# Two transformer blocks on one core: where the operands of the feed-forward matmuls lie in the on-chip memory

## The chip, the core and the metric

One core of a Trainium2 chip runs the whole program. The metric is the device time of one execution in microseconds. The kernel before took 2065.55 us (median of 3 runs, 2063.72 to 2067.26).

## The reference

A sequence of 256 positions with 1,024 features goes through two blocks in float32. The first block has an RWKV-7 and an RG-LRU branch, a cross attention and a feed-forward with a short convolution (`conv_ffn`). The second block runs twice (two layers), each with a gated feed-forward, a token mixing of three attention forms, a cross attention and a second gated feed-forward. What the change touches are the feed-forwards:

```
def swiglu(h, w13, w2):
    gate, up = jnp.split(h @ w13, 2, axis=-1)
    return (jax.nn.silu(gate) * up) @ w2

x = x + 0.5 * rms_norm_2(swiglu(rms_norm_2(x, g0), w13, w2), g1)   # D_MODEL 1024, D_FF 2816
```

There are four of these gated feed-forwards (two per layer) and one `conv_ffn` of the same sizes.

## The kernel before, in words

**Products in three parts.** Every large product is made of three matmuls in a reduced-precision form of float32: an operand is split into a high part (a cast on ScalarE, line 209) and a low part (a subtraction on VectorE, line 210), and `mm3` (lines 240 to 244) adds high x high, high x low and low x high in the accumulator. In the profile the lines 242, 243 and 244 are these three. A name with h or l at its end is a high or low part; in `out<-in,in` the moving operand comes first and the stationary one second.

**Weights.** `weights` (213) loads a raw tile of 128 x 1,024 floats from SP's queue and splits it into `wh` and `wl`, in pool `wp` with three buffers each. `wcols` (229) gives the eight row tiles of a column block.

**Feed-forward** (`ffn`, 405). `norm_T` (355) normalises and transposes the activations into eight slices xt of 128 x 256 (high and low), held in four of the ten 4,096-byte buffers of pool `sl4`. Then comes a loop over 11 hidden blocks j of 256 columns: `proj_fm` (255) makes gate and up, 48 matmuls of 256 columns each, with the weights stationary and xt moving; `hidden` applies the gate; the result is split into hh and hl. One step later `down` (276) multiplies the hidden block j-1, now stationary in pieces of 128 x 128, with the down weights, now moving with 512 columns: 24 matmuls a block into four accumulators. The last three of the 22 down rows keep their weights in a pool `tail` of their own (281 to 303) and are multiplied together. `fill` (two key/value projections of the memory for the next cross attention, `kv_job` 1007) gives TensorE work while the activations are normalised.

**Cross attention** (`cross`, 488) has its own pool: kv (8 buffers, keys, values and, later, the heads' outputs), `gap0` (64 bytes), queries, p, `gap1` (384 bytes), pt; the pool `tail` for its down projection (`down_all`, 305) is opened behind it. The heads' outputs are the stationary operand of that down projection. In the mixing block (`mix2`, 1356) the stationary operand of the down projection is `mh`/`ml`, in `sl4` (`merge`, 173).

**Order of work.** The instructions of each engine are ordered by a scheduler that follows the program's order and priorities with a model of the time; waits follow from the data and from the reuse of buffers. Nothing in the order is written by hand around the change. Pools are laid behind one another in the order in which they are opened, and tiles in a pool in the order in which their names first appear.

**Places.** Modulo 256 bytes: the `sl4` buffers start at 0. Line 119 puts a pad of 64 bytes behind them, so that `wp` and the pools opened later (`ff`, `tail`, `cr`) start at 64; `mix2` starts its pool with a pad of 448. Tiles of the loops are multiples of 1,024 bytes long, so distances are the same for every buffer of a name. So xt (in `sl4`) is 64 bytes below its weights or, counted upwards, 192 above; hh and hl (in `ff`) are at the same place as the down weights; mh and ml are 64 bytes below theirs; the heads' outputs in `cross` are level with the weights in `wp`, and 64 above those in `tail`, which start 448 bytes on.

Of the kernel before, what the change touches and what calls it, by code (L numbers as in the profile page):

```python
# [110 lines left out]
class Core:  # L111
# [290 lines left out]
        return xs  # L402


    def ffn(self, xs, gsrc, w_in, w_out, hidden, fill=None):
        xt = self.norm_T(xs, gsrc)
        if fill:
            self.parts = PK
            fill()
        self.parts = PF  # L410
        pend = []
        with self.pool("ff", 3) as pool, self.pool("tail", FTAIL) as tail, self.pool("raws", 7) as raws:
            self.phase(pool)
            acc, step = self.down_steps(w_out, 2 * NJ, tail, FTAIL)
            for j in range(NJ + 1):
                self.raws = raws if j else self.wp
                if j < NJ:
                    bg = self.proj_fm(self.wcols(w_in, j * 256, 256), xt)
                    bu = self.proj_fm(self.wcols(w_in, FF + j * 256, 256), xt)
                    hd = hidden(j, bg, bu)  # L420
                    p = Pair(self.R("hh", [128, 2, T], F32R), self.R("hl", [128, 2, T], F32R))
                    self.split(hd, p.h, p.l)
                    pend.append(p)
                if j:
                    for i in range(2):
                        step(2 * (j - 1) + i, pend[j - 1][:, i, :])
        self.raws = self.wp
        return acc
# [59 lines left out]
    def cross(self, xs, gx, w_q, w_o, mt, w_kv, raw, mid=None, ntail=TAIL):  # L488

        nc = self.nc  # L490
        self.parts = PC
        R = self.R
        xt = self.norm_T(xs, gx)
        after = self.last_copy
        kv = {}

        def get(i):

            got = []
            if i in raw:  # L500
                for r in raw[i]:
                    p = Pair(R("kvh", [128, 2, T], F32R, 8), R("kvl", [128, 2, T], F32R, 8))
                    with self.tc.issue_after(after):
                        self.split(r, p.h, p.l)
                    got.append([p[:, 0, :], p[:, 1, :]])
            else:
                got = [self.fm_pair(b, "kv", 8) for b in self.kv_chunk(mt, w_kv, i)]
            if i < 4:
                kv[i] = got[0]
            else:  # L510
                for j in range(2):
                    kv[2 * i - 4 + j] = [got[0][j], got[1][j]]

        outs = {}
        sc, pt = {}, {}

        def scores(h):
            if h == 0:
                R("gap0", [128, 16], bufs=1)
            q = self.fm_pair(self.proj_fm(self.wcols(w_q, h * 256, 256), xt), "cq", 2)  # L520
            b = self.bank("c")
            v = b.rearrange("p (a c) -> p a c", a=2)
            for t in range(2):
                for i in range(2):
                    self.mm3(v[:, t, :], q[i][:, t * 128:(t + 1) * 128], kv[h][i], t == 0 and i == 0, t == 1 and i == 1)
            p, rc = self.softmax_bank(v, 2, 256 ** -0.5, R("p", [128, 2, T], bufs=4))
            for t in range(2):
                nc.vector.tensor_scalar(out=p[:, t, :], in0=p[:, t, :], scalar1=rc[:, t:t + 1], scalar2=None,
                                        op0=ALU.mult)
            sc[h] = p  # L530

        def values(h):
            p = sc[h]
            b = self.bank("c")
            for kt in range(2):
                for t in range(2):
                    o = kt * T + t * 128
                    nc.tensor.transpose(b[:, o:o + 128], p[:, t, kt * 128:(kt + 1) * 128], self.ident)
            if h == 0:
                R("gap1", [128, 96], bufs=1)  # L540
            pt = self.fm_pair(b, "pt", 2)
            b = self.bank("c")
            for i in range(2):
                for kt in range(2):
                    self.mm3(b[:, i * T:(i + 1) * T], kv[4 + h][kt][:, i * 128:(i + 1) * 128], pt[kt],
                             i == 0 and kt == 0, i == 1 and kt == 1)
            outs[h] = self.fm_pair(b, "kv", 8)

        for i in range(6):
            if i not in raw:  # L550
                get(i)
        for h in range(4 + LAG):
            if h < 4:
                for i in (h, 4 + h // 2):
                    if i in raw and (i < 4 or h % 2 == 0):
                        get(i)
                scores(h)
            if h >= LAG:
                values(h - LAG)
        if mid:  # L560
            mid()
        return self.down_all([outs[h][i] for h in range(4) for i in range(2)], w_o, ntail)
# [456 lines left out]
    def run(self, out):  # L1019
        a, nc = self.a, self.nc  # L1020
        n2 = a["cross_norms_2"]
        side = ExitStack()
        mem = {}

        def open_side():
            self.rawp = side.enter_context(self.pool("raw", side="right"))
            self.pad(self.rawp, 224)
            mem["R"] = self.mkR(side.enter_context(self.pool("mt", side="right")))

        def early(pool):  # L1030
            mem["mt"] = self.norm_T(self.load_x(a["mem"][0]), a["norm_mem_g"][0])
            mem["raw"] = {i: [pool.tile([128, 2, T], F32, name="raw_b1%d" % i)] for i in range(NEARLY)}
            self.kv_job(mem["mt"], a["w_ckv"][0], mem["raw"])(8)

        def prepare(l):

            mt = self.mem_T(a["mem_2"][0], n2[l, 2], mem["R"])
            rt = lambda n: self.rawp.tile([128, 2, T], F32, tag=n, name=n)
            raw = {i: [rt("raw%d%d" % (i, j)) for j in range(1 if i < 4 else 2)] for i in range(5)}
            mem.update(mt=mt, raw=raw, fill=self.kv_job(mt, a["cross_wkv_2"][l], raw))  # L1040

        fill = lambda n: mem["fill"](n)

        def start_ffn():
            fill(2)
            self.rope_tables()

        with self.pool("b1") as pool:
            with self.pool("gt") as gp:
                xs = self.mix1(gp, lambda names: self.load_const(names, pool), lambda: early(pool), open_side)  # L1050
            with self.pool("cr") as cp:
                self.phase(cp)
                acc = self.cross(xs, a["norm_x_g"][0], a["w_cq"][0], a["w_co"][0], mem["mt"], a["w_ckv"][0],
                                 mem["raw"], mid=lambda: prepare(0))
            xs = self.residual(xs, acc)
            acc = self.ffn(xs, a["norm_ffn_g"][0], a["w_ffn_in"][0], a["w_ffn_out"][0], self.conv_hidden,
                           start_ffn)
        xs = self.final_norm(self.residual(xs, acc), a["norm_final_g"])
        with self.pool("b2") as pool:
            self.load_const(["ret"], pool)  # L1060
            for l in range(2):
                acc = self.ffn(xs, a["ffn1_norms_2"][l, 0], a["ffn1_w13_2"][l], a["ffn1_w2_2"][l], self.swiglu_hidden,
                               lambda: fill(2))
                xs = self.residual(xs, acc, a["ffn1_norms_2"][l, 1], 0.5)
                acc = self.mix2(l, xs, lambda: fill(6))
                xs = self.residual(xs, acc, a["mix_norms_2"][l, 1])
                with self.pool("cr") as cp:
                    self.phase(cp)
                    acc = self.cross(xs, n2[l, 0], a["cross_wq_2"][l], a["cross_wo_2"][l], mem["mt"],
                                     a["cross_wkv_2"][l], mem["raw"], mid=(lambda: prepare(1)) if l == 0 else side.close, ntail=TAILS[l])  # L1070
                xs = self.residual(xs, acc, n2[l, 1])
                acc = self.ffn(xs, a["ffn2_norms_2"][l, 0], a["ffn2_w13_2"][l], a["ffn2_w2_2"][l], self.swiglu_hidden,
                               (lambda: fill(2)) if l == 0 else None)
                xs = self.residual(xs, acc, a["ffn2_norms_2"][l, 1], 0.5)
        for t in range(2):
            for h in range(2):
                s = slice(h * 512, (h + 1) * 512)
                nc.sync.dma_start(out=out[t * 128:(t + 1) * 128, s], in_=xs[t][:, s])
# [377 lines left out]
```

## Time and profile before

| | |
|---|---|
| median of 3 runs | 2065.55 us |
| profiled execution | 2068.93 us |
| its span, first to last instruction | 2067.2 us |
| TensorE matmul busy | 2006.2 us (97%) |
| VectorE, ScalarE busy | 1320.1 us (64%), 1093.7 us (53%) |
| mean granted TensorE clock | 0.991 |

Busy times of TensorE are made from reported starts and modelled ends: matmuls are pipelined, and a reported duration is longer than the distance to the next start. The distance between starts is what a matmul costs in a row of them. The timeline gives the start of each instruction, its duration, and the idle time before it in brackets where there is any.

### The profile page before, as it was taken

What the parts mean: (1) busy time and instruction counts of PE and PEld (TensorE: products, weight loads), DVE (VectorE), ACT (ScalarE), POOL (GpSimd) and SP (SyncE); (2) the same over time, 40 slices, a digit from 0 to 9 for tenths busy, and PEclk for the clock granted to TensorE, in tenths of its full rate; (3) what the DMA queues carried; (4) which work ended last, traced back from release to release, by engine and by line L of the source; (5) the groups of instructions that cost most, each with busy time, mean ns of one, the idle gap of its engine ahead of it and who ended that gap; (6) DMA issues with size and microseconds to landing.
All of it is one profiled execution on the core that took longest, in us unless ns stands there. A gap on an engine that the chain in (4) does not pass through costs nothing.

```text
span 2067.2 us, 36137 instructions
## 1 busy us (share of the span) xinstructions
PE 2006.2 (97%) x14508; PEld 1843.3 (89%) x14508; DVE 1320.1 (64%) x2183; ACT 1093.7 (53%) x2014; POOL 45.6 (2%) x65
## 2 busy tenths in 40 slices
PE   7999999999999999999999999999999999998998
PEld 6989978899999998789988999999987799888997
DVE  6896567766675556765667555755577656665555
ACT  5763245655564455654456544644466544554444
POOL 0000000000000001000000000000000000000000
PEclk9999999999999999999999999999999999999999
DMA  6432255666666655436655666656644456545663
GB/s 199 145 119 83 93 183 188 221 184 191 188 218 193 185 163 154 136 108 184 200 194 194 212 189 190 208 175 192 190 121 148 123 163 185 192 154 174 193 191 105
DMA packets 259033, 352.92 MB, mean 171 GB/s; under 512 B 12336, under 2 KB 214448, under 8 KB 258864
## 3 DMA queue, kind: packets, MB, share of 16 engines
q1 hardware_dynamic: 258864, 350.60, 55.1%
q8 instruction: 114, 1.87, 0.4%
q14 instruction: 55, 0.45, 0.1%
HBM read 349.50 MB, written 1.05 MB: 170 GB/s over the span
## 4 chain that ended last, share of the span: by engine, by line
PE 86%; DVE 5%; DMA 4%; ACT 3%; issue 1%; POOL 0%; SPq 0%; DVEq 0%; POOLq 0%; ACTq 0%
PE bp L242 20%; PE bp L243 20%; PE bp L244 20%; PE acc L242 6%; PE acc L243 6%; PE acc L244 6%; PE a L247 3%; DVE wl L210 2%; ACT wh L209 2%; PE bc L247 1%; DMA raw<-in_w_in_dram 1%; PE bc L1131 1%; PE bc L368 1%; DMA raw<-in_cross_wkv_dram 1%; DMA g<-in_cross_norms_dram 1%
## 5 line engine op out<-in xcount | busy, mean ns | idle before, releaser
L210 DVE TENSOR_TENSOR wl<-raw,wh 128x512 fp32r<-128x512 f32 (+2 forms) x1082 | 796.7, 773 | 532.9 <-ACT wh L209 520.8
L209 ACT CAST wh<-raw 128x512 fp32r<-128x512 f32 (+2 forms) x1082 | 699.7, 688 | 713.2 <-PE bp L243 496.8
L242 PE MATMUL bp<-xth,wh 128*128 128x256 f32 x2704 | 763.8, 283 | 8.3 <-ACT xth L209 3.8
L244 PE MATMUL bp<-xth,wl 128*128 128x256 f32 x2704 | 760.7, 282 | 5.4 <-DVE wl L210 5.4
L243 PE MATMUL bp<-xtl,wh 128*128 128x256 f32 x2704 | 761.3, 282 | 2.9 <-DVE xtl L210 2.9
L242 PEld LDWEIGHTS bp<-xth,wh 128*128 128x128 f32 x2704 | 513.2, 190 | 19.4 <-ACT xth L209 6.5
L244 PEld LDWEIGHTS bp<-xth,wl 128*128 128x128 f32 x2704 | 515.5, 191 | 11.3 <-DVE wl L210 6.4
L243 PEld LDWEIGHTS bp<-xtl,wh 128*128 128x128 f32 x2704 | 512.8, 190 | 6.8 <-DVE xtl L210 4.1
L243 PE MATMUL acc<-wl,hh 128*128 128x512 f32 x440 | 171.8, 390 | 0.0
L244 PE MATMUL acc<-wh,hl 128*128 128x512 f32 x440 | 170.5, 390 | 0.0
L242 PE MATMUL acc<-wh,hh 128*128 128x512 f32 x440 | 142.0, 391 | 0.0
L242 PE MATMUL bp<-wh,xth 128*128 128x512 f32 (+1 forms) x256 | 98.7, 400 | 2.3 <-DVE tmd L1126 1.4
L243 PE MATMUL bp<-wl,xth 128*128 128x512 f32 (+1 forms) x256 | 100.5, 396 | 0.0
L244 PE MATMUL bp<-wh,xtl 128*128 128x512 f32 (+1 forms) x256 | 99.2, 393 | 0.0
L243 PEld LDWEIGHTS acc<-wl,hh 128*128 128x128 f32 x440 | 82.7, 188 | 14.4
L244 PEld LDWEIGHTS acc<-wh,hl 128*128 128x128 f32 x440 | 82.6, 188 | 14.5
L242 PEld LDWEIGHTS acc<-wh,hh 128*128 128x128 f32 x440 | 79.1, 188 | 13.3
L343 POOL TENSOR_TENSOR rr<-rv,mhalf 128x1 f32<-128x1 f32 x46 | 30.2, 658 | 1656.8 <-DVE rv L341 1656.4
L242 PEld LDWEIGHTS bp<-wh,xth 128*128 128x128 f32 x256 | 47.3, 188 | 13.3 <-ACT tmd L1276 2.1
L243 PEld LDWEIGHTS bp<-wl,xth 128*128 128x128 f32 x256 | 48.2, 188 | 9.2 <-DVE wl L210 0.8
L244 PEld LDWEIGHTS bp<-wh,xtl 128*128 128x128 f32 x256 | 48.2, 188 | 8.4
L244 PE MATMUL bp<-bh,wl 128*128 128x256 f32 x192 | 54.0, 281 | 0.0
(377 smaller groups left out, 2582.7 us busy)
## 6 DMA issues: line engine op xcount, KB each, us to landing
raw<-in_ffn_w_dram SPq DMA_DIRECT2D x264, 512.0 KB, 4.4
raw<-in_w_in_dram SPq DMA_DIRECT2D x134, 512.0 KB, 3.8
raw<-in_w_ffn_in_dram SPq DMA_DIRECT2D x44, 512.0 KB, 4.6
raw<-in_cross_wkv_dram SPq DMA_DIRECT2D x32, 512.0 KB, 4.2
raw<-in_w_branch_dram SPq DMA_DIRECT2D x24, 512.0 KB, 3.9
raw<-in_w_ffn_out_dram SPq DMA_DIRECT2D x22, 512.0 KB, 4.2
raw<-in_w_ckv_dram SPq DMA_DIRECT2D x16, 512.0 KB, 4.3
raw<-in_w_out_dram SPq DMA_DIRECT2D x16, 512.0 KB, 4.3
```

The costliest lines, as they stand in the source:

```text
L209: first = self.nc.scalar.copy(out=h, in_=src)
L210: self.nc.vector.tensor_tensor(out=l, in0=src, in1=h.bitcast(F32), op=ALU.subtract)
L242: mm(out, a.h, b.h, start=start, stop=False, skip_group_check=True)
L243: mm(out, a.h, b.l, start=False, stop=False, skip_group_check=True)
L244: mm(out, a.l, b.h, start=False, stop=stop, skip_group_check=True)
L247: self.nc.tensor.matmul(out, a, b, start=start, stop=stop, skip_group_check=True)
L343: nc.gpsimd.tensor_tensor(out=r, in0=v, in1=self.mhalf[:, :1], op=ALU.pow)
L368: nc.tensor.transpose(b[:, j * 128:(j + 1) * 128], xn[:, k * 128:(k + 1) * 128], self.ident)
L1131: self.nc.tensor.transpose(b[0:s.shape[1], i * 128:(i + 1) * 128], s, self.ident)
```

## The change

Three things. The gated feed-forwards get their xt in four buffers of a pool of their own (4,352 bytes each, opened ahead of the hidden buffers), starting 208, 200, 176 and 184 bytes further than the weights modulo 256 (first feed-forward of layer 0 and of layer 1, second feed-forward of layer 0 and of layer 1). In all five feed-forwards 192 bytes are put ahead of hh and hl and 64 behind them, so that hh and hl stand 64 bytes below the down weights and all that follows keeps its place modulo 256. In the three cross attentions 64 bytes are put behind pt, so that the tail weights of their down projection move up by 64 bytes. No instruction of the computation is added or taken away.

```diff
-    def ffn(self, xs, gsrc, w_in, w_out, hidden, fill=None):
-        xt = self.norm_T(xs, gsrc)
+    def ffn(self, xs, gsrc, w_in, w_out, hidden, fill=None, off=None):
+
+        if off is not None:
+            with self.pool("xt") as pool:
+                tile = lambda n: pool.tile([128, 1088], F32R, name=n)[:, off // 4:off // 4 + 1024].rearrange(
+                    "p (k c) -> p k c", k=4)
+                xt = [Pair(tile("fxh%d" % i), tile("fxl%d" % i)) for i in range(2)]
+                return self.ffn_on(self.norm_T(xs, gsrc, xt), w_in, w_out, hidden, fill)
+        return self.ffn_on(self.norm_T(xs, gsrc), w_in, w_out, hidden, fill)
+
+    def ffn_on(self, xt, w_in, w_out, hidden, fill):
...
                     hd = hidden(j, bg, bu)
+                    if j == 0:
+                        self.R("gap0", [128, 48], bufs=1)
                     p = Pair(self.R("hh", [128, 2, T], F32R), self.R("hl", [128, 2, T], F32R))
+                    if j == 0:
+                        self.R("gap1", [128, 16], bufs=1)
...
             pt = self.fm_pair(b, "pt", 2)
+            if h == 0:
+                R("gap2", [128, 16], bufs=1)
...
                 acc = self.ffn(xs, a["ffn1_norms_2"][l, 0], a["ffn1_w13_2"][l], a["ffn1_w2_2"][l], self.swiglu_hidden,
-                               lambda: fill(2))
+                               lambda: fill(2), off=(208, 200)[l])
...
                 acc = self.ffn(xs, a["ffn2_norms_2"][l, 0], a["ffn2_w13_2"][l], a["ffn2_w2_2"][l], self.swiglu_hidden,
-                               (lambda: fill(2)) if l == 0 else None)
+                               (lambda: fill(2)) if l == 0 else None, off=(176, 184)[l])
```

## Rows read from the trace of the kernel before

**Rows 1.** The page's busy times, and its chain by engine.

```profile
PE 2006.2 (97%) x14508; PEld 1843.3 (89%) x14508; DVE 1320.1 (64%) x2183; ACT 1093.7 (53%) x2014; POOL 45.6 (2%) x65
...
PE 86%; DVE 5%; DMA 4%; ACT 3%; issue 1%; POOL 0%; SPq 0%; DVEq 0%; POOLq 0%; ACTq 0%
```

**Rows 2.** TensorE's groups by shape: count, busy us, mean ns of one, idle before.

```profile
L242 PE MATMUL bp<-xth,wh 128*128 128x256 f32 x2704 | 763.8, 283 | 8.3 <-ACT xth L209 3.8 <-ACT wh L209 1.4 <-DVE wl L210 1.1
...
L243 PE MATMUL acc<-wl,hh 128*128 128x512 f32 x440 | 171.8, 390 | 0.0
...
L243 PE MATMUL acc<-wl,mh 128*128 128x512 f32 x96 | 38.0, 397 | 0.0
```

**Rows 3.** Two stretches: us, PE busy (instructions), granted clock, DMA share, GB/s.

```profile
1145.00:1160.00 15.00, 15.00 (x135) 1.00 0.62 192
1206.00:1212.00 6.00, 6.00 (x53) 1.00 0.55 174
```

**Rows 4.** Timeline of TensorE, one block: start us, us, line, operation, count.

```profile
1204.84 0.28 PE L244 MATMUL bp<-xth,wl 128*128 128x256 f32 x1
...
1212.62 0.63 PE L242 MATMUL acc<-wh,hh 128*128 128x512 f32 x2
1213.08 0.28 PE L244 MATMUL bp<-xth,wl 128*128 128x256 f32 x1
1213.20 0.28 PE L242 MATMUL bp<-xth,wh 128*128 128x256 f32 x1
1213.32 0.28 PE L243 MATMUL bp<-xtl,wh 128*128 128x256 f32 x1
1213.43 0.28 PE L244 MATMUL bp<-xth,wl 128*128 128x256 f32 x1
...
1216.27 0.39 PE L243 MATMUL acc<-wl,hh 128*128 128x512 f32 x1
...
1220.36 0.28 PE L242 MATMUL bp<-xth,wh 128*128 128x256 f32 x1
...
1220.60 0.39 PE L243 MATMUL acc<-wl,hh 128*128 128x512 f32 x1
...
1221.52 0.28 PE L244 MATMUL bp<-xth,wl 128*128 128x256 f32 x1
```

**Rows 5.** Timeline, downs of the mixing block: first and last of 31 in order.

```profile
1762.15 0.40 PE L243 MATMUL acc<-wl,mh 128*128 128x512 f32 x1
...
1769.15 0.40 PE L243 MATMUL acc<-wl,mh 128*128 128x512 f32 x1
```

**Rows 6.** Timeline, last tail downs of a cross attention and the matmuls behind them.

```profile
1856.86 0.39 PE L243 MATMUL acc<-wl,kvh 128*128 128x512 f32 x1
1857.09 0.39 PE L244 MATMUL acc<-wh,kvl 128*128 128x512 f32 x1
1857.32 0.28 PE L242 MATMUL bc<-pth,kvh 128*128 128x256 f32 x1
1857.44 0.28 PE L243 MATMUL bc<-ptl,kvh 128*128 128x256 f32 x1
1857.56 0.28 PE L244 MATMUL bc<-pth,kvl 128*128 128x256 f32 x1
1857.67 0.28 PE L242 MATMUL bc<-pth,kvh 128*128 128x256 f32 x1
...
1858.58 0.28 PE L244 MATMUL bc<-pth,kvl 128*128 128x256 f32 x1
```

**Rows 7.** Timeline, token-major projection: first and last of 29 in order.

```profile
318.46 0.39 PE L244 MATMUL bp<-wh,xtl 128*128 128x512 f32 x1
...
324.87 0.39 PE L244 MATMUL bp<-wh,xtl 128*128 128x512 f32 x1
```

**Rows 8.** Timeline, first of three tail downs and the matmul behind them.

```profile
1848.28 0.39 PE L242 MATMUL acc<-wh,kvh 128*128 128x512 f32 x1
...
1848.97 0.28 PE L242 MATMUL bc<-pth,kvh 128*128 128x256 f32 x1
```

**Rows 9.** Waits of SP's queue: us in total, times, longest.

```profile
SPq L1171 <- PE acc L244: 13.1, 2, 6.5
```

## The prediction

> **What bounds the kernel now.** I read the engines' busy time and the chain first [rows 1]: TensorE is busy for 97% of the span and makes 86% of the chain, so only what TensorE issues, and how fast, can move the end. The profiled execution took 2068.93 us, 2067.2 of it span; the sums below are made against it, and it stands 3.4 us (0.16%) above the median of 2065.55, on which the forecast is put. From no change the measurement can tell about 0.2%, some 4.1 us.
>
> Next the groups by shape [rows 2]. A 256-column matmul of the up projections ("up": activations move, weights are stationary) is reported with 283 ns, a 512-column one of the feed-forward down projection ("down": weights move, activations are stationary) with 390, and a down of the mixing block with 397, at one shape. These times overlap, so what counts is start to start. In the timeline of one block of a feed-forward [rows 4] 66 ups start between 1204.84 and 1212.62, one per 117.9 ns; then 2 downs; then 28 ups between 1213.08 and 1216.27, the first three 120, 120 and 110 ns apart and the rest 113.3 or so; then 18 downs in 4.09 us, 227 each. Same instructions, same buffers, two paces. It is not the clock: the granted clock is 1.00 of 2.4 GHz in a fast stretch and in a slow one [rows 3]. And it isn't waiting, as no idle time stands in those rows. Call 113.3 fast and 117.8 slow.
>
> What flips it? After the 18 downs, which have settled at 227, the ups start slow at once (1220.36 to 1220.60: 120 each) and stay slow for the 66 of the next block. After 2 downs that follow slow ups and haven't settled yet (230 each), the ups are fast three matmuls later. So the pace is a state handed on from one kind to the next, and the settled 227 is what hands on the slow one.
>
> The distances, by the code: everything behind the pad of 64 bytes lies 64 off the s4 buffers, modulo 256. So ups read activations 64 bytes from their weights; feed-forward downs read hh and hl at distance 0; the mixing block's downs have their stationary in s4, 64 bytes short of the moving weights, which is the distance that the feed-forward downs get. Those run at 7.00 us for 30 [rows 5], 233.3 each, and don't settle lower. The last downs of a cross attention, 64 bytes off in the other direction, run at 233 too, and there the ups behind them start with 120, 120, 110 and are fast from then on [rows 6]. A third row at the new distance: token-major projections, 28 in 6.41 us, 228.9 each [rows 7].
>
> **The change part by part.**
>
> 1. *Feed-forward downs from 0 to 64 bytes, five feed-forwards.* A block has 24 downs. Now they take 0.46 (2) + 4.09 (18) + 0.92 (4) = 5.47 us [rows 4]. At 233.3 they take 5.60, +0.13 us; at 228.9, 5.49, +0.02. Which of the two? The 233.3 rows were entered from slow ups, the 228.9 row not. The nearest to what comes after is three 64-byte downs behind fast ups, 1848.28 to 1848.97, 230 each [rows 8]. Both ends are kept; I take the middle, +0.07 per block.
>
> 2. *Ups behind such downs.* If the 64-byte downs hand on the fast state, as in [rows 6], all 96 ups of a block are fast, not 28: 68 x (117.8 - 113.3) = 0.31 us less. Each of the three entries costs the first three ups about 10 ns in all; one of them is paid today, so +0.02. Sum per block: -0.31 + 0.02 + 0.07 = -0.22 us, between -0.16 and -0.27. The block of 16.68 us stands ten times in each of five feed-forwards: 50 x -0.22 = -11 us (-8 to -13.5). The 24 downs after the last up of each feed-forward have no ups to help: 5 x 24 x 2 to 6.7 ns, +0.2 to +0.8, take +0.5. The first 164 ups come before any down and stay as they are.
>
> 3. *Own buffers, 208, 200, 176 and 184.* Today the activations stand at 192 (64 short of 256), so they move by +16, +8, -16, -8 bytes. No row shows an up at such a distance. Nearest rows: ups at 64, fast or slow. Lower bound, fast at every one, which is in term 2 already: 0. Upper bound, slow at every one, whatever the downs hand on: the rival below. I take 0, since the rows are 8 and 16 bytes away and the larger distances, 0 and 64, cost the downs at most 6.7 ns. Of instructions none is added: the same four casts and four subtractions write the activations.
>
> 4. *Four s4 slots free; the pool of 17,408 bytes pushes the hidden buffers, tail and raw weights up.* A first write now waits for older tiles of that region, all read before the norm that feeds it can run: 0 to +1 us in all. One wait gets shorter: SP stands 13.1 us in two waits at the mixing block's gain load, behind the last downs [rows 9], because that tile lies over the third hh; it will lie over the activations and sg, free when ups and hidden steps are done, some 6 us earlier. Behind it in the queue stand further gain loads and the next raw weights, which wait for their own raw buffers; TensorE has the key and value matmuls as cover there. Taken as 0; bounds -1 and +1.
>
> 5. *The 64 bytes after pt in cross.* kv is at distance 0 from the ordinary down weights, and the tail weights lie 448 further, so 64 off; with 64 more they are at 0. Tail downs: 3 + 3 + 6 rows of 12, 144 in all, 233.3 to 227, -0.9 us. Against it, ups behind them may turn slow: five groups of 12 at 4.5 ns, +0.3. Net -0.6, bounds -0.9 and +0.9 (the next feed-forward's first ups too).
>
> Sum: -11 + 0.5 + 0 + 0 - 0.6 = -11.1, from -7.5 to -15. On the median: 2065.55 - 11.1 = about 2054 us. DVE (64% busy) and the loads have slack for a TensorE 0.6% faster; if that cover were gone the ups would wait for wl, which now costs 5 us or so in all.
>
> **The rivals.**
>
> *The gated ups turn slow for good (slower).* At 48 to 80 bytes the slow pattern may be the only stable one. Place: the four gated feed-forwards. Price per block: 28 ups x 4.5 = +0.13, downs entered from slow ups, so at 233.3 as in [rows 5], +0.13: +0.26 x 40 = +10.4 us; the first 164 ups of three of them, where they are fast now, +2.2; the first feed-forward gains its 1.6 to 2.7; term 2's last downs +0.8. About +11, 2077 us. It decides once more than about half of the gated blocks are slow. For: nothing measured at these distances, and the change has a different one in each. Against: the state depends on what comes before, at one and the same distance [rows 4].
>
> *Half and half.* Two of the four gated offsets keep the ups fast, two don't: three feed-forwards at -2.2, two at +2.6, first ups +1.1: about 0, 2065.
>
> *Everything locks at its floor.* Fast ups hand the downs 226.7 also at 64 bytes: per block -0.31 - 0.03 = -0.34, 50 times -17: 2048 us. Against it, [rows 5] never settle there.
>
> *Distance counts for nothing*, the difference between 227 and 233 being something else about the mixing block: no change, 2065.5. Against it: [rows 6, 7], at 64 bytes and other stages, aren't at 227 either. The Trainium skill says so too, in its own way ("TensorE: Matmul & The Clock Gate", section "Part 2: What happens when you issue a matmul"): TensorE has two independent read ports, one for the streaming operand and one for the weights; by that the sum would be 0. The paces above don't agree with it.
>
> *Rows that start off their grid cost a little more.* If each moving row of 1,024 bytes at 200 and 184 touched one piece of 16 bytes in 65 more, an up would take 113.3/64 = 1.8 ns longer, 1,056 x 2 x 1.8 = +3.7 us, 2058. The Trainium skill gives a ground for it ("SBUF — State Buffer", section "Specifications (TRN2)"): lines of 16 bytes, with a penalty for each new line. No run here has an operand off 64 bytes, so the trace says neither.
>
> **How the numbers follow.** Fast ups in all or nearly all blocks: 0.53 (2050 to 2058); everything at its floor: 0.08; off-grid rows on top of fast ups: 0.05, 2058; half and half: 0.12, of it the larger part within 0.2%; no effect: 0.07; gated ups slow: 0.15. Faster by over 0.2% (below 2061.4): 0.53 + 0.08 + 0.05, less 0.03 for small gains, = 0.63. Within 0.2%: 0.07 + 0.08 + 0.03 = 0.18. Slower: 0.15 + 0.04 = 0.19. The predicted time is that of the likeliest case, 2054 us; its own range is 2050 to 2058. The range for 8 in 10 leaves out the worse half of the slow case and most of the floor case: 2047 to 2071.
>
> **What would show it.** Right: in the timeline of a gated block, ups 113.3 apart after each group of downs, downs at 229 to 233, block length 16.4 to 16.5 us against 16.68; the mean of bp<-xth,wh falls from 283 towards 278, that of acc<-wl,hh rises from 390 to 392 to 397. The first feed-forward, whose ups keep their distance, shows term 2 alone. Wrong: ups at 117.8 behind 64-byte downs there; a third pace in the gated ones; blocks that differ from one gated feed-forward to the next by more than 0.1 us; or TensorE waiting at the start of a feed-forward for xt.

## The result, and the profile after

The changed kernel took 2084.44 us (median of 4 runs, 2077.73 to 2085.69) against 2066.41 of the kernel before (4 runs): ratio 1.0085, 95% interval 1.0070 to 1.0099. It is slower by 18 us, where 11 less were forecast, and above the range. The profiled execution is the run of 2085.69, span 2083.9.

The page of the changed kernel, the lines that answer to [rows 1, 2]: engines' busy time; the chain by engine; TensorE's groups. The activations of the gated feed-forwards are now fxh and fxl, so that these groups hold them alone.

```profile
PE 2022.7 (97%) x14508; PEld 1858.3 (89%) x14508; DVE 1320.5 (63%) x2183; ACT 1093.1 (52%) x2014; POOL 45.4 (2%) x65
...
PE 87%; DVE 5%; DMA 3%; ACT 3%; issue 1%; POOL 0%; SPq 0%; DVEq 0%; POOLq 0%; ACTq 0%
...
L243 PE MATMUL bp<-fxl,wh 128*128 128x256 f32 x1408 | 399.1, 284 | 0.9 <-DVE fxl L210 0.9
...
L243 PE MATMUL acc<-wl,hh 128*128 128x512 f32 x440 | 172.8, 393 | 0.0
```

The bound is the same, TensorE at 97% with the same 14,508 matmuls, and its busy time rose by 16.5 us, the span by 16.7. So the same instructions take longer. The gated ups are reported with 283 or 284 ns, where the prediction looked for 278, and the downs with 393, inside its 392 to 397.

The timeline of one block of a gated feed-forward (layer 1, activations at 200) answers to [rows 4]; columns as there.

```profile
1396.81 0.28 PE L244 MATMUL bp<-fxh,wl 128*128 128x256 f32 x1
...
1404.74 0.63 PE L242 MATMUL acc<-wh,hh 128*128 128x512 f32 x2
1405.21 0.28 PE L244 MATMUL bp<-fxh,wl 128*128 128x256 f32 x1
...
1408.59 0.40 PE L243 MATMUL acc<-wl,hh 128*128 128x512 f32 x1
...
1412.71 0.28 PE L242 MATMUL bp<-fxh,wh 128*128 128x256 f32 x1
...
1413.89 0.28 PE L244 MATMUL bp<-fxh,wl 128*128 128x256 f32 x1
```

The 66 ups take 7.93 us, 120.2 ns each, and the 28 behind two downs 3.38 us, 120.7 each: neither 113.3 nor 117.8 but a third, slower pace, and it is there behind every group of downs. The 18 downs take 4.12 us, 228.9 each. The block is 17.08 us long; it was 16.68.

All starts of the trace give the table below: the mean distance from one up to the next, in ns (pauses of 140 ns and more left out), and in brackets where the activations stand, in bytes above the weights.

| ups of | before | after |
|---|---|---|
| conv feed-forward | 116.7 (192) | 116.8 (192) |
| first gated, layer 0 | 116.0 (192) | 119.2 (208) |
| second gated, layer 0 | 116.0 (192) | 119.3 (176) |
| first gated, layer 1 | 116.8 (192) | 120.3 (200) |
| second gated, layer 1 | 116.0 (192) | 120.0 (184) |

With 1,056 ups in each, the four gated rows make 3.4 + 3.5 + 3.7 + 4.2 = 14.8 us. The downs of the five rose from 228.3 to 229.9 on the mean: 1,320 x 1.65 ns = 2.2 us. A third piece is in neither: at the start of the first gated feed-forward TensorE idles. The timeline of that start, its rows with idle time, of the changed kernel:

```profile
607.69 1.25 PE L368 MATMUL bc<-c_ident,xn 128*128 128x128 f32 x8 [1.64 <-DVE fxl L210]
609.14 0.51 PE L242 MATMUL bp<-fxh,wh 128*128 128x256 f32 x2 [0.20 <-ACT fxh L209]
610.09 0.39 PE L243 MATMUL bp<-fxl,wh 128*128 128x256 f32 x1 [0.44 <-DVE fxl L210]
```

and of the kernel before:

```profile
605.14 0.38 PE L243 MATMUL bp<-xtl,wh 128*128 128x256 f32 x1 [0.64 <-DVE xtl L210]
```

That is 2.28 us of idle time against 0.64, 1.6 us more, and the prediction had named it as a sign of being wrong ("TensorE waiting at the start of a feed-forward for xt"). From the last down of the conv feed-forward to the first down of this one it is 34.7 us against 32.4. The three pieces make 18.6 us, where the span rose by 16.7; the other stages differ by up to 2.5 us either way between the two profiles, and do so between kernels that share them.

### The profile page after: what moved, and what is told of

The parts are those of the page before. It is cut to its first block, busy times and chain, and to the rows that moved or that the text cites. A ratio compares the mean times of both kernels' runs of the same rounds, so it can differ in the third digit from the quotient of the medians.

```text
span 2083.9 us, 36129 instructions
## 1 busy us (share of the span) xinstructions
PE 2022.7 (97%) x14508; PEld 1858.3 (89%) x14508; DVE 1320.5 (63%) x2183; ACT 1093.1 (52%) x2014; POOL 45.4 (2%) x65
## 4 chain that ended last, share of the span: by engine, by line
PE 87%; DVE 5%; DMA 3%; ACT 3%; issue 1%; POOL 0%; SPq 0%; DVEq 0%; POOLq 0%; ACTq 0%
PE bp L242 20%; PE bp L243 20%; PE bp L244 20%; PE acc L242 7%; PE acc L243 6%; PE acc L244 6%; PE a L247 3%; DVE wl L210 2%; PE bc L247 1%; ACT wh L209 1%; DMA raw<-in_w_in_dram 1%; PE bc L368 1%; PE bc L1146 1%; DMA raw<-in_cross_wo_dram 1%; DMA raw<-in_cross_wkv_dram 0%
## 5 line engine op out<-in xcount | busy, mean ns | idle before, releaser
L243 PE MATMUL bp<-fxl,wh 128*128 128x256 f32 x1408 | 399.1, 284 | 0.9 <-DVE fxl L210 0.9
L242 PE MATMUL bp<-fxh,wh 128*128 128x256 f32 x1408 | 397.9, 283 | 1.4 <-ACT fxh L209 1.4
L244 PE MATMUL bp<-fxh,wl 128*128 128x256 f32 x1408 | 397.0, 283 | 0.0
L242 PE MATMUL bp<-xth,wh 128*128 128x256 f32 x1296 | 369.3, 285 | 7.2 <-ACT xth L209 2.7
L244 PE MATMUL bp<-xth,wl 128*128 128x256 f32 x1296 | 367.0, 284 | 5.5 <-DVE wl L210 5.3
L243 PE MATMUL bp<-xtl,wh 128*128 128x256 f32 x1296 | 366.3, 283 | 1.4 <-DVE xtl L210 1.4
L243 PEld LDWEIGHTS bp<-fxl,wh 128*128 128x128 f32 x1408 | 267.8, 190 | 3.3 <-DVE fxl L210 1.8
L244 PEld LDWEIGHTS bp<-fxh,wl 128*128 128x128 f32 x1408 | 266.0, 189 | 3.2
L244 PEld LDWEIGHTS bp<-xth,wl 128*128 128x128 f32 x1296 | 246.9, 191 | 8.6 <-DVE wl L210 7.1
L243 PEld LDWEIGHTS bp<-xtl,wh 128*128 128x128 f32 x1296 | 246.4, 190 | 3.1 <-DVE xtl L210 1.8
```

The source lines that it names most:

```text
L242: mm(out, a.h, b.h, start=start, stop=False, skip_group_check=True)
L243: mm(out, a.h, b.l, start=False, stop=False, skip_group_check=True)
L244: mm(out, a.l, b.h, start=False, stop=stop, skip_group_check=True)
```

## The experiments

Eleven kernels, one of them twice, in three groups of four rows each; each group ran on one chip beside the kernel before (2065.91 us in the first, 2063.88 in the second, 2064.58 in the third). All numbers of paces below are worked out as in the table above. Of the kernels that ran once only the paces are used.

| kernel | us (runs) | ratio to before, 95% |
|---|---|---|
| own buffers at 192 | 2062.14 (10) | 0.9979, 0.9970 to 0.9988 |
| downs alone | 2055.79 (5) | 0.9953, 0.9941 to 0.9966 |
| offsets alone | 2082.00 (4) | 1.0079, 1.0064 to 1.0094 |
| offsets 224, 160, 128, 0 | 2078.72 (1) | one run |
| offsets 64, 32, 96, 196 | 2072.97 (1) | one run |
| downs and gap2 | 2057.81 (12) | 0.9972, 0.9961 to 0.9983 |
| downs and hand-over | 2054.15 (6) | 0.9952, 0.9939 to 0.9965 |
| own buffers at 192 in three | 2058.30 (12) | 0.9975, 0.9967 to 0.9984 |
| grid | 2068.93 (1) | one run |
| downs alone, again | 2059.00 (10) | 0.9975, 0.9965 to 0.9985 |
| downs and hand-over in conv | 2055.33 (5) | 0.9959, 0.9946 to 0.9972 |
| hand-over, downs at 0 | 2062.83 (11) | 0.9991, 0.9981 to 1.0000 |

One kernel stands twice in it, at 0.9953 and 0.9975: differences under some 5 us between groups are not read from the times, but from the stages of the traces, which repeat to 0.3 us.

**Is it the distance, the buffers, or the downs?** The change with its activations back at 192, in their own buffers:

```diff
-                               lambda: fill(2), off=(208, 200)[l])
+                               lambda: fill(2), off=(192, 192)[l])
...
-                               (lambda: fill(2)) if l == 0 else None, off=(176, 184)[l])
+                               (lambda: fill(2)) if l == 0 else None, off=(192, 192)[l])
```

> The changed kernel with its four own buffers, but all at 192 bytes from the weights, the distance of before; the downs stay at 64 bytes. Theory 1 (the distance sets the pace of the ups): the gated ups fall from 119 to 120 ns back to 116 to 117, the downs stay at 229 to 231, total 2067 to 2071 us (before 2066.4 plus the 2 us of the downs). Theory 2 (the buffers' new place, or what the new pool moves, slows them): ups stay at 119 to 120, total 2081 to 2085 us. Theory 3 (64-byte downs hand the ups a slow state): also 2081 to 2085 us.

Its gated ups on the page, where the changed kernel had 399.1 and 284:

```profile
L243 PE MATMUL bp<-fxl,wh 128*128 128x256 f32 x1408 | 391.6, 278 | 1.1 <-DVE fxl L210 1.1
```

From start to start the gated ups fell to 114.0 and 114.0 in layer 0 and 114.5 and 114.7 in layer 1, below those of before, and the time to 2062.1 us, 5 less than the first theory gave; the next kernel shows why. The distance is the cause of the loss, neither the buffers nor the downs: 16 or 8 bytes make 22 us between two kernels that differ in nothing else (1.0085 and 0.9979 of the kernel before). The own buffers are 4,352 bytes apart, 17 times 256, so a high and a low part stand an odd multiple of 256 from each other; at 192 they read alike (in the first gated feed-forward 114.4 and 113.9 for the high parts, 113.7 for the low one), which bears out counting the distance modulo 256.

Of the change only gap0 and gap1:

```diff
                     hd = hidden(j, bg, bu)
+                    if j == 0:
+                        self.R("gap0", [128, 48], bufs=1)
                     p = Pair(self.R("hh", [128, 2, T], F32R), self.R("hl", [128, 2, T], F32R))
+                    if j == 0:
+                        self.R("gap1", [128, 16], bufs=1)
```

> The kernel before with the 192 and 64 bytes around hh and hl alone: only the downs of the five feed-forwards change their distance, to 64 bytes. Theories 1 and 2: downs from 228.3 to about 230 ns each, ups as before (116 to 117 ns), total up by 1 to 4 us, 2067 to 2070. Theory 3: ups at 119 to 120 ns in the gated feed-forwards, total 2080 us or more. My forecast of before the result: ups at 113 to 114 and 8 to 13 us less.

One block of a gated feed-forward in that kernel (timeline):

```profile
646.33 0.28 PE L244 MATMUL bp<-xth,wl 128*128 128x256 f32 x1
...
653.83 0.62 PE L242 MATMUL acc<-wh,hh 128*128 128x512 f32 x2
654.29 0.28 PE L244 MATMUL bp<-xth,wl 128*128 128x256 f32 x1
...
657.48 0.39 PE L243 MATMUL acc<-wl,hh 128*128 128x512 f32 x1
...
662.76 0.28 PE L244 MATMUL bp<-xth,wl 128*128 128x256 f32 x1
```

Here the 66 ups take 7.50 us, 113.6 each: the 64-byte downs hand on the 113.3 pace, as the prediction's second term had it, and the block is 16.43 us long, inside its 16.4 to 16.5. The kernel took 2055.8 us, 10.1 less than the kernel before, and 5.6 less when it ran again in the third group. The granted clock is that of the slow block; two stretches within the 66 ups, of the changed kernel and of this one (us, PE busy and instructions, granted clock, DMA share, GB/s):

```profile
1397.00:1404.00 7.00, 7.00 (x60) 1.00 0.55 167
```

```profile
646.50:653.50 7.00, 7.00 (x64) 1.00 0.61 176
```

The gated ups read 114.0 to 114.5, but the conv feed-forward's stayed at 116.8. Then the change without its three gaps, so that the downs stay at 0 (the diff of the change without the lines of gap0, gap1 and gap2):

> The changed kernel without the bytes around hh and hl and behind pt: downs back at distance 0, own buffers at 208, 200, 176 and 184 kept. Theories 1 and 2: gated ups at 119 to 120 ns, total 2079 to 2083 us, so nearly all of the loss. Theory 3: ups back at 116 to 117 ns, total 2065 to 2068 us.

Gated ups at 118.7, 119.2, 120.2 and 119.9 (at 208, 176, 200 and 184) and 2082.0 us, inside the 2079 to 2083 of the first two theories: the offsets alone make nearly all of the loss, whatever the downs hand on.

**Which distances?** That kernel, with other offsets:

```diff
-off=(208, 200)[l]
+off=(224, 160)[l]
...
-off=(176, 184)[l]
+off=(128, 0)[l]
```

> As the run before it (downs at 0), with the four own buffers at 224, 160 (first feed-forward of layer 0, layer 1) and 128, 0 (second ones). Theory 1: the means of the ups differ between the four by 1 ns or more; if what counts is whether the distance is a multiple of 64, then 116 to 118 ns at 128 and 0 and 119 or more at 224 and 160. Theory 2: 119 to 120 ns in all four.

and with (64, 32) and (96, 196):

> The four offsets alone (no gaps, so the downs stay at distance 0), set to 64 and 96 bytes (first gated feed-forward of layer 0, second of layer 0) and 32 and 196 bytes (first and second of layer 1). The sum of the ups of a gated feed-forward was 122.3 us before and 125 to 127 us at 128 to 224 (without 192) and 0. Theory 'one distance': only 64 bytes below the weights (192 counted upwards) has the fast pace, so all four places read 118 to 120.5 ns a matmul and none 113.3, 196 among them; time 2076 to 2084. Rival 'either side': what counts is 64 bytes without regard to which operand lies above, so the feed-forward at 64 reads 116 ns with stretches of 113.3 as before, the other three 118 to 120; about 3 us less, 2074 to 2080. Rival 'nearly 64 will do': 196 differs by 4 bytes only and reads 116 as before, the other three 118 to 120.

| bytes above the weights | 0 | 32 | 64 | 96 | 128 | 160 | 176 | 184 | 192 | 196 | 200 | 208 | 224 |
|---|---|---|---|---|---|---|---|---|---|---|---|---|---|
| mean ns of an up | 119.6 | 116.7 | 117.7 | 119.9 | 118.7 | 118.7 | 119.3 | 120.0 | 114.0 to 116.8 | 121.6 | 120.3 | 118.7 to 119.2 | 118.3 |

Each distance but 192 was seen in one or two feed-forwards. That multiples of 64 are fast is out: 0 and 128 read 119.6 and 118.7. "Nearly 64 will do" falls hardest: 4 bytes off is the slowest of all. "One distance" missed at 32, where the ups go round in a pattern of 113 to 120 with a mean of 116.7, level with before. And it missed at 64 above, where the ups sit at 117.8, the slow pace of 192, but for one stretch behind the first two downs:

```profile
625.25 0.62 PE L242 MATMUL acc<-wh,hh 128*128 128x512 f32 x2
625.70 0.28 PE L244 MATMUL bp<-fxh,wl 128*128 128x256 f32 x1
...
628.87 0.39 PE L243 MATMUL acc<-wl,hh 128*128 128x512 f32 x1
```

These 28 ups take 3.17 us, 113.2 each. So 64 on either side has both paces, and no other distance of the table shows a stretch of 28 ups or more at 113.3. What differs between the two sides is the hand-over: behind two downs at distance 0 the 28 ups were fast in 1 of 10 blocks at 64 above and in 49 of 50 at 192 in the kernel before. Whether downs at 64 bytes would turn more of them at 64 above was not run, so "either side" stays open.

**The distance, or the place?** Own buffers at 192 as in the first experiment, and

```diff
-        self.pad(p("gap", 1), 64)
+        self.pad(p("gap", 1), 96)
```

> The change with own buffers 192 bytes from the weights in all four gated feed-forwards, and the pad behind the shared buffers 96 bytes in place of 64: weights at 96 modulo 256, the own buffers at 32, their distance 64 as before; the shared buffers stay at 0, so that the conv feed-forward and every other product that reads from them have a distance of 96. Theory 'the distance between the two operands counts, not the place of either': the gated feed-forwards' ups read 114.0 to 114.7 with stretches of 113.3, as with the weights at 64; the conv feed-forward's ups rise from 116.8 to 118 to 121 (118.7 was read at 96 in another feed-forward). Rival 'the operands must start at a multiple of 64': the gated ups read 118 to 121 too. The time as a whole says little, since every other stage has another distance: 2070 to 2095 by the first, 2095 to 2115 by the second.

Two groups of its page, the gated ups and all the others:

```profile
L243 PE MATMUL bp<-fxl,wh 128*128 128x256 f32 x1408 | 391.7, 278 | 1.0 <-DVE fxl L210 1.0
...
L243 PE MATMUL bp<-xtl,wh 128*128 128x256 f32 x1296 | 366.6, 283 | 2.0 <-DVE xtl L210 2.0
```

With weights at 96 and activations at 32 modulo 256, 64 apart, the gated ups read 114.0 to 114.7, as with both on multiples of 64. The conv feed-forward, whose activations now stand 160 above the weights, read 118.6, where 118.7 was read at 160 in another feed-forward and another place. The distance counts; that the place does not is shown at this one other place. (The expectation called conv's distance 96, counted upwards from the activations to the weights.)

**Where are the 3 us at the first gated start?** Own buffers at 192 in the three other gated feed-forwards, no gap2:

```diff
-off=(208, 200)[l]
+off=(None, 192)[l]
```

> The downs at 64 bytes and own buffers for the activations in three of the four gated feed-forwards, at 192 bytes as before; the first gated feed-forward keeps its activations in the shared buffers. TensorE's order is that of the kernel with the downs alone (2055.8 us); with own buffers in all four (2062.1 us) it differed in 51 places around the start of the first gated feed-forward. Theory 'the 6 us of own buffers lie at that one start' (VectorE works in another order there, TensorE waits 1.9 us and then runs at the lower clock for some 20 matmuls): 2056 to 2058. Rival 'each own pool costs at its own start': 2055.8 + 3/4 x 6.3 = 2060.5.

The start of the first gated feed-forward, its one row with idle time:

```profile
603.04 0.38 PE L243 MATMUL bp<-xtl,wh 128*128 128x256 f32 x1 [0.69 <-DVE xtl L210]
```

From the last conv down to its first down it is 32.3 us, as in the kernel with the downs alone; it is 32.3 to 33.1 in all kernels without own buffers there, the longer ones where its first 164 ups run at 117.8, and 34.7 to 37.3 in the six with them. At the start of the first gated feed-forward of layer 1, own buffers or not, it is 33.6 to 34.2. So the cost lies at that one start, by the traces; the times decide nothing, as 2058.3 lies between the two theories and between the two times of the kernel with the downs alone (2055.8 and 2059.0). What happens there is in VectorE's rows of the kernel before:

```profile
600.68 1.28 DVE L210 TENSOR_TENSOR xtl<-bc,xth 128x512 fp32r<-128x512 f32 x2
601.88 1.41 DVE L351 SCALAR_TENSOR_TENSOR xn<-xn,rr,g 128x512 f32<-128x512 f32 x2
```

and of the changed kernel:

```profile
602.78 1.28 DVE L210 TENSOR_TENSOR wl<-raw,wh 128x512 fp32r<-128x512 f32 x2
...
604.41 1.29 DVE L210 TENSOR_TENSOR wl<-raw,wh 128x512 fp32r<-128x512 f32 x2 [0.28 <-ACT wh L209]
...
605.62 1.41 DVE L351 SCALAR_TENSOR_TENSOR xn<-xn,rr,g 128x512 f32<-128x512 f32 x2
606.95 1.28 DVE L210 TENSOR_TENSOR fxl<-bc,fxh 128x512 fp32r<-128x512 f32 x2
```

In the changed kernel VectorE makes four low parts of weights ahead of the second half's normalisation (line 351) and of the low parts of the first half's activations (fxl). TensorE's transposes of the second half, the row at 607.69 above, need the first and, by the trace, wait for the second, which came last. In four of the six kernels with own buffers there, the pause was followed by a stretch at a lower granted clock, a mean of 0.50 to 0.63 over 4 us; 0.50 is 1.2 GHz, the lower of the clock's two levels. In the first experiment (columns as in the stretches above):

```profile
608.00:612.00 4.00, 4.00 (x21) 0.57 0.38 131
```

In the other two, the changed kernel and the one with offsets 64, 32, 96 and 196, the clock stayed at 1.00 behind a pause of the same length (1.6 us for the transposes in all six); these are the starts of 34.7 and 34.8 us, the four others took 35.4 to 37.3.

**gap2.** The kernel with the downs alone, and

```diff
             pt = self.fm_pair(b, "pt", 2)
+            if h == 0:
+                R("gap2", [128, 16], bufs=1)
```

> The kernel with the downs of the feed-forwards at 64 bytes alone (2055.8 us), and the 64 bytes behind pt in the three cross attentions added; nothing else differs. The prediction's term 5 says -0.6 us for the three (-0.9 to +0.9): 2055.2. Rival 'the place counts for nothing outside the feed-forwards': 2055.8. Rival 'the changed kernel's cross attentions were longer by it' (the first read 79.9 against 83.0 before, the third no difference): down to 2053 for one of them. A difference under 1 us can't be told from none here.

The kernel with the downs alone ran once more, beside the third group:

> The kernel with the downs of the feed-forwards at 64 bytes alone, once more beside the two kernels below on the same chip: 0.9953 of the kernel before (0.9941 to 0.9966) as measured.

For the kernel with gap2, 0.9972 stands between the two readings of the kernel without it: no difference that the times can tell. In the traces the tail downs, some 120 at 64 bytes, read about 233 without it; with it all downs of the cross attentions are at 0 and read 229.5. That is some 0.5 us, the prediction's size.

**Why did conv gain nothing?** In the kernel with the downs alone, one block of the conv feed-forward:

```profile
482.04 0.28 PE L242 MATMUL bp<-xth,wh 128*128 128x256 f32 x1
...
490.05 0.63 PE L242 MATMUL acc<-wh,hh 128*128 128x512 f32 x2
490.52 0.28 PE L244 MATMUL bp<-xth,wl 128*128 128x256 f32 x1
...
493.71 0.39 PE L243 MATMUL acc<-wl,hh 128*128 128x512 f32 x1
...
498.75 0.28 PE L242 MATMUL bp<-xth,wh 128*128 128x256 f32 x1
```

68 ups in 8.01 us (117.8), 2 downs, 28 ups in 3.19 (113.9), 22 downs in a row. A gated block has 18 downs, 2 ups, 4 downs. The 117.8 pace behind 64-byte downs is a sign of being wrong that the prediction had named for this very feed-forward. The reading to test: settled downs hand on the 117.8 pace at 64 bytes too, and it takes a few downs behind slow ups to turn it. For that the last three downs of a step are held back behind the first three ups of the next block:

```diff
+                up = self.mm3(...)
+                self.release(up)
...
+            if hold and half:
+                self.held.append(one)
...
-                    self.down(acc, t, hid, w, k == 0, False)
+                    self.down(acc, t, hid, w, k == 0, False, self.holds and k % 2 == 1 and t == 1)
...
+    def release(self, up=None):
+        if self.held and up is not None:
+            with self.tc.issue_after(up.ins):
+                for f in self.held:
+                    f()
```

> The kernel with the downs at 64 bytes alone (2055.8 us), and in the conv feed-forward and in the one block of each gated one where 22 downs stood in a row ahead of 68 ups, the last three of these downs are held back behind the first three ups of the next block (22 downs, 68 ups becomes 19 downs, 3 ups, 3 downs, 65 ups); no instruction is added. Theory 'the hand-over decides': downs that have run on to their settled pace hand on the slow state, three downs that come behind a few slow ups hand on the fast one. Then the 65 ups read 113.3 in place of 117.8: 65 x 4.5 ns = 0.29 us in each of 9 conv blocks and 4 gated ones, -3.8 us, against some 13 x 0.05 us for three downs at 233 in place of 228: -3.1 us, 2052.7; the conv feed-forward's ups fall from 116.8 to 114.2 on the mean. Rival 'conv has something else of its own' (its longer chain of VectorE and ScalarE work, its place in memory): the ups stay at 116.8 and the time at 2055.8 or a little above, for 26 more changes between the two kinds of matmul.

The conv feed-forward of that kernel (its lines stand one further down, 243 to 245):

```profile
483.11 0.28 PE L243 MATMUL bp<-xth,wh 128*128 128x256 f32 x1
...
483.46 0.40 PE L243 MATMUL acc<-wh,hh 128*128 128x512 f32 x1
483.70 0.39 PE L244 MATMUL acc<-wl,hh 128*128 128x512 f32 x1
483.93 0.40 PE L245 MATMUL acc<-wh,hl 128*128 128x512 f32 x1
484.17 0.28 PE L243 MATMUL bp<-xth,wh 128*128 128x256 f32 x1
...
491.54 0.62 PE L243 MATMUL acc<-wh,hh 128*128 128x512 f32 x2
```

Three ups, three downs in 0.71 us (237 each), then 65 ups in 7.37 us: 113.4 each. All 13 blocks so changed did the same. The conv ups fell to 114.3, its stage from 165.4 to 162.9 us, the same instructions in another order, and the four gated stages by 0.3 us each. In conv alone:

> The downs at 64 bytes and three downs held back behind three ups in the conv feed-forward alone (the gated ones in the order of the kernel with the downs alone). With the held downs in the gated ones too the conv feed-forward's ups fell from 116.8 to 114.3 and its stage by 2.5 us. Theory 'hand-over': the same 2.5 us here, so 2.5 us less than the kernel with the downs alone in the same call. Rival 'what conv gains is lost at what follows': no difference between the two.

162.9 us again. The time is 3.7 us below that of the kernel with the downs alone beside it (2.5 expected), but the two intervals overlap (0.9946 to 0.9972 and 0.9965 to 0.9985), so it is the stage that shows the gain. And the same order at distance 0:

> The kernel before, downs at distance 0, with the order of 19 downs, 3 ups, 3 downs, 65 ups in the conv feed-forward and in one block of each gated one. Theory 'the 64 bytes set what downs hand on': in the kernel before, two downs at distance 0 handed on the fast state and four handed on the slow one; three at distance 0 read 234 233 236 or so and hand on the slow one, so conv stays at 116.7 and the time at that of before, or up to 1 us above for the unsettled downs. Rival 'the order alone does it': conv falls to 114.3, 2.5 to 3.5 us less than before.

```profile
484.32 0.28 PE L243 MATMUL bp<-xth,wh 128*128 128x256 f32 x1
...
484.67 0.39 PE L243 MATMUL acc<-wh,hh 128*128 128x512 f32 x1
484.90 0.39 PE L244 MATMUL acc<-wl,hh 128*128 128x512 f32 x1
485.13 0.39 PE L245 MATMUL acc<-wh,hl 128*128 128x512 f32 x1
485.35 0.28 PE L243 MATMUL bp<-xth,wh 128*128 128x256 f32 x1
...
493.01 0.63 PE L243 MATMUL acc<-wh,hh 128*128 128x512 f32 x2
```

Here the three downs take 0.68 us, 227 each, settled at once, and the 65 ups 7.66 us, 117.8 each. The downs read 227 and not the 234 that was expected. It was so in 12 of the 13 blocks with this order. The one that differs is the last of them in conv:

```profile
567.86 0.34 PE L245 MATMUL bp<-xth,wl 128*128 128x256 f32 x1
568.03 0.39 PE L243 MATMUL acc<-wh,hh 128*128 128x512 f32 x1
...
568.74 0.28 PE L243 MATMUL bp<-xth,wh 128*128 128x256 f32 x1
...
576.12 0.63 PE L243 MATMUL acc<-wh,hh 128*128 128x512 f32 x2
```

Here the first down starts 0.18 us after the third up, some 60 ns later than in the other blocks; the three downs then take 0.71 us, as at 64 bytes, and the 65 ups 7.38 us, 113.5 each. So downs at distance 0 can hand on the fast pace too, when they don't settle at once. The order alone rarely does it; with the 64 bytes it did it every time. Nor are a few 64-byte downs behind slow ups always enough: in four kernels the first two downs of one gated feed-forward, behind 164 slow ups, left the next 28 at 117.9. What the state is made of is not shown.

The lowest time is that of the kernel with the downs at 64 bytes and three held back in conv and the gated ones, 2054.15 us, 0.9952; from the first reading of the downs alone, 0.9953, the times can't tell it.

## Why the prediction was wrong

**Term 3 failed**, "I take 0, since the rows are 8 and 16 bytes away", and with it its upper bound, "slow at every one". The ups at 208, 200, 176 and 184 have no 113.3 pace, and their pace is worse than the slow one: 119.2 to 120.3 against 114.0 to 114.7 at 192 beside the same downs, 4 x 1,056 x 5.4 ns = 23 us. The 22 us between the change and its copy at 192 say the same. The two paces of one distance were taken for the two ends of what distance can do; the rows only held distances 0 and 64, so they bounded nothing at 48 to 80. The rival "gated ups turn slow for good" had place and sign right, at 0.15, and its price, +11 us, too low: it knew no third pace, and half of it was for downs at 233.3, which read 229.9.

**Term 2** was right in mechanism, and its size off by a count. It said ten blocks in each of five feed-forwards, 50 x -0.22. The block of [rows 4] stands eight times in each of the four gated ones; the two others there, and all ten in conv, end with 22 downs in a row and hand on the 117.8 pace. 32 x -0.22 = -7.0, where the stages of the kernel with the downs alone give, for the gated ups, 1,056 x (2.0 + 2.0 + 2.3 + 2.0) ns = -8.8, for the conv ups +0.1 and for all downs +1.7: -7.0. By the times the downs alone gained 10.1 and 5.6 us. In the changed kernel none of it is left: the gated ups lost it to their distance, and in conv, whose ups kept theirs, 22 downs in a row stood ahead of the ups.

**Term 1**, +0.07 a block, +3.5 us with 50, was taken between 228.9 and 233.3; measured 229.6 in the kernel with the downs alone, 229.1 to 231.0 after, 2.2 us in all. **Term 4** was right in that SP's wait of [rows 9] is gone and gains nothing: the weights' loads behind it start 7 us after the last down as before. It missed the 2 to 5 us at the first gated start, where the other buffers changed the order on VectorE. **Term 5** is right in the traces and too small for the times.

Of the rivals on distance, "counts for nothing" is out. The Trainium skill ("TensorE: Matmul & The Clock Gate", section "Part 2: What happens when you issue a matmul") has independent read ports for the two operands, from which the prediction worked out a sum of 0; the traces don't agree with that sum, as the gated ups read 114.0 to 114.7 at 192 and 119.2 to 120.3 at the change's distances with nothing else changed. Whether the ports are the reason no run shows. Of rows off their grid: in the changed kernel 200 and 184 read 0.9 ns more than 208 and 176, and 196 read another 1.5 more. The Trainium skill's lines of 16 bytes ("SBUF — State Buffer", section "Specifications (TRN2)") fit the first, not the second, as 184, 196 and 200 are all off such lines; and 96, a multiple of 16, read 119.9. Each was seen once or twice, so this stays open.

## What to carry to other kernels

Where TensorE is the bound and matmuls stand in rows without idle time, read the distance between starts by stretch: several paces of one instruction at the full granted clock point to where its operands lie and to what ran before. A price seen at two distances says nothing about a third, however near; leave an operand that has a fast state where it is, or try it on one feed-forward first. And before a price per block is multiplied, count in the trace how often that very order of instructions occurs.

## What the runs showed that was not expected

- Distance modulo 256 between moving and stationary operand sets the pace of 256-column matmuls: 113.3 or 117.8 at 192 and at 64, means of 116.7 to 121.6 at the other distances; 4 bytes off the good distance was the worst, 121.6. At the one other place that was tried, the grid kernel, the pair read the same at the same distance. Why is not shown by any run.
- The pace at 192 is handed on through the other kind of matmul: three downs at 64 bytes behind three slow ups turned the next 65 from 117.8 to 113.4 in all 13 blocks of one kernel; the same three at 0 did so in 1 of 13.
- A pause of some 2 us of TensorE (idle rows as above) was followed by a mean granted clock of 0.50 to 0.63 over 4 us in four kernels and by the full clock in two others.
